# The high halves of 38 probability tiles, from VectorE to ScalarE, in a sparse-attention layer

## The chip, the cores and the metric

The kernel runs on one core of a Trainium2 chip. A core has TensorE (matmuls, PE in the profile, its weight loads PEld), VectorE (DVE), ScalarE (ACT), GpSimd (POOL) and SyncE (SP, which issues most of the DMAs). The metric is the device time of one execution in microseconds; several runs are made and their median is taken.

## The reference

One inference step of a layer with two token mixers. What matters here is mixer A on the prompt (1024 tokens, 8 heads of 64 in 2 groups g of 4, which share keys and values):

```
s_s = einsum('bqgrd,bgqnld->bqgrnl', qg, k_sel) * scale     # selected blocks of 64 keys
p_s = softmax(where(m_s, s_s, NEG));  o_s = p_s @ v_sel
s_w = einsum('bqgrd,bkgd->bqgrk', qg, kw) * scale           # window of 512 keys
p_w = softmax(where(m_w, s_w, NEG));  o_w = p_w @ vw
o_a = gw[..., 0] * o_c + gw[..., 1] * o_s + gw[..., 2] * o_w
```

A third branch, o_c, works on compressed keys and gives the scores by which the blocks are selected. The mixer's output is gated (SiLU), projected, merged with mixer B through sigmoid gates (g_a, g_b), and projected once more (w_out). All of it is float32.

## The kernel before

To be as exact as float32 and as fast as the quicker format FR (float32r), the kernel splits an operand into a high half, rounded to FR, and a low half, the rest, and sums the products of the halves. A split is two instructions: a copy into FR (the high half) and a subtraction (the low half).

The attention goes over 16 tiles (g, i), i being a block of 128 queries. For each, `front` makes the queries' transposes (R, R2), finds the maxima of the scores (matmuls into PSUM banks of the tag mx, in which the masks of the edges are added by an FR matmul of an identity, `ident_r`, with a table, `edges`; VectorE reduces them to bm and wm) and selects the blocks (imp, BT). `scores` then goes through the spans (w, k) of the tile, first the window's (w = 1), then the selected blocks' (w = 0), 132 in all: two matmuls into a PSUM bank st (two banks), an exponential on ScalarE into pt (four buffers), and, where the span lies on an edge, a mask on GpSimd (40 of the 132). For each span `low` splits the probabilities into `p2[:, 0]` and `p2[:, 1]`, and `outputs` adds three matmuls with the values into a bank pv. `weigh` and `close` scale and sum the branches (sr, u, f). `n` is the span's number in its tile, and n % 3 says which engine makes the halves: the high half is made by VectorE where n % 3 = 2 (38 spans) and by ScalarE elsewhere (94); the low half by GpSimd where n % 3 = 1 (44) and by VectorE elsewhere (88).

The profile leaves out the numbers of buffers, so that p2 reads p, R2 reads R, L1 and L2 read L, and s4 and s8 read s. All instructions carry line 216, the proxy that records them, so they are told apart by their tiles.

The order of all instructions is set beforehand by a planner (`Plan`): every stream of work is a generator that yields what it waits for; the planner estimates each instruction's cost by engine and size, and takes next the stream whose data are ready first by its own account. Matmuls of the projections and gates (`ct_proj`, tiles mm<-hh,c0h and the like, 128x344, six at a time) are the filler: they are taken when the attention has nothing ready. When the last tile of g = 1 is closed, the merge is opened: `products` loads back what was spilled and splits it into xh and xl, and `merge_job` multiplies these with w_br_b and then w_br_a; the output projection follows. The engines run in order, each on its own list, and wait for each other by semaphores.

Of the kernel before, what the change touches and what calls it, by code (L numbers as in the profile page):

```python
# [13 lines left out]
AF = mybir.ActivationFunctionType  # L14
# [244 lines left out]
def nsa_gmlp_step(ctx: ExitStack, tc: tile.TileContext, a: dict):  # L259
    nc = tc.nc  # L260
    plan = Plan()
    dve, act, pool, pe, sp = (plan.engine(e, n) for e, n in (
        (nc.vector, "dve"), (nc.scalar, "act"), (nc.gpsimd, "pool"), (nc.tensor, "pe"), (nc.sync, "sp")))
# [1446 lines left out]
    def scores():  # L1710

        for g, i in TILES:
            yield lambda: (g, i) in got and "blocks" in built
            R, R2, pgT = got.pop((g, i))
            pgTs[g, i] = pgT
            Rf, R2f = R.rearrange("p r q -> p (r q)"), R2.rearrange("p r q -> p (r q)")
            for n, (w, k) in enumerate(spans(i)):
                yield lambda: waiting[0] < PT_BUFS
                yield bank_free("st")
                waiting[0] += 1  # L1720
                s = bank("st")
                sl = slice(k * 128, k * 128 + 128)
                pe.matmul(s, lhsT=L1[g, w][:, sl], rhs=Rf, start=True, stop=False)
                pe.matmul(s, lhsT=L2[g, w][:, sl], rhs=R2f, start=False, stop=True)
                pt = areg.tile([128, 512], F32, name="pt", bufs=PT_BUFS)
                act.activation(pt, s, AF.Exp, scale=0.125)
                if k == i or w and k == i - 4:
                    sign = 1 if k == i else -1
                    pool.affine_select(out=pt, in_=pt, pattern=[[0, 4], [sign, 128]], compare_op=OP.is_ge, fill=0.0,
                                       base=min(sign, 0), channel_multiplier=-sign)  # L1730
                plan.add(low(g, i, n, pt), 0)
            scored[0] += 1

    def low(g, i, n, pt):

        yield pt
        yield lambda: flying[0] < P_BUFS
        flying[0] += 1
        p2 = areg.tile([128, 2, 512], FR, name="p2", bufs=P_BUFS)
        if n % 3 in HI_DVE:  # L1740
            dve.tensor_copy(p2[:, 0], pt)
        else:
            act.activation(p2[:, 0], pt, AF.Copy)
        yield p2[:, 0]
        (pool if n % 3 in ON_POOL else dve).tensor_tensor(p2[:, 1], pt, p2[:, 0].bitcast(F32), op=OP.subtract)
        waiting[0] -= 1
        cut[g, i, n] = p2
# [24 lines left out]
            plan.add(close(g, i, pgTs.pop((g, i)), o), 0)  # L1772

    ON_POOL = (1,)
    HI_DVE = (2,)
    pgTs, cut = {}, {}
    waiting, flying, scored, open_ = [0], [0], [0], [0]

# [250 lines left out]
```

## Time and profile before

| | before |
|---|---|
| median of 3 runs (lowest to highest) | 1042.48 us (1041.79 to 1043.07) |
| profiled execution: time, span | 1042.65 us, 1041.0 us |
| PE busy | 1017.1 us, 98% |
| PEld busy | 887.8 us, 85% |
| DVE busy | 653.5 us, 63% |
| ACT busy | 468.6 us, 45% |
| POOL busy | 306.7 us, 29% |
| granted TensorE clock, mean | 0.998 |

The profile is one execution. Busy times are unions over an engine's instructions; a matmul's record runs from its start to its modelled end and overlaps the next, so a full PE row tells that work was always under way, not that none of it stood. The rows of waits are what tells that. An engine's idle time before an instruction is put down to the instruction that released it.

### The profile page before, as it was taken

The numbers are of one execution on the slowest core, as the hardware profiler recorded it, in microseconds if no ns is written. First come the engines' busy times: TensorE is split into PE (matmuls) and PEld (weight loads), VectorE is DVE, ScalarE is ACT, GpSimd is POOL, SyncE is SP. The second block draws the span as 40 slices with busy tenths as digits, with TensorE's granted clock in tenths as the row PEclk, the third lists the DMA queues.
The fourth block names the chain that finished last, engine by engine and source line by source line (L and its number), as shares of the span: only waits on it lengthen the run. The fifth ranks groups of instructions, "written<-read, shape, count | busy, mean of one in ns | idle before, by whom it ended". The sixth has DMA issues, their size and how long they took to land. (4 is left out here: it accounts for less than half of the span.)

```text
span 1041.0 us, 16320 instructions
## 1 busy us (share of the span) xinstructions
PE 1017.1 (98%) x5711; PEld 887.8 (85%) x5711; DVE 653.5 (63%) x1371; ACT 468.6 (45%) x984; POOL 306.7 (29%) x332
## 2 busy tenths in 40 slices
PE   7999999999999999999999999999999999999998
PEld 2589977879999999987888888878789999998776
DVE  4676786454668757477788568896843345575322
ACT  5774232001322245777766676667675331232000
POOL 0443574555231110013334332433343000251000
PEclk9999999999999999999999999999999999999999
DMA  9735451203874745421311121211123586554321
GB/s 320 249 115 175 135 183 43 71 21 113 285 216 143 261 147 195 132 67 55 92 56 46 57 72 48 63 29 51 30 68 89 184 246 202 173 159 143 123 90 63
DMA packets 106311, 130.33 MB, mean 125 GB/s; under 512 B 27299, under 2 KB 71525, under 8 KB 106230
## 3 DMA queue, kind: packets, MB, share of 16 engines
q1 hardware_dynamic: 101622, 112.52, 34.4%
q0 software_dynamic: 4608, 16.78, 5.3%
q8 instruction: 45, 0.74, 0.3%
q14 instruction: 36, 0.29, 0.1%
HBM read 98.95 MB, written 30.23 MB: 124 GB/s over the span
## 5 line engine op out<-in xcount | busy, mean ns | idle before, releaser
L216 PE MATMUL pv<-p,vv 128*128 128x512 f32 (+1 forms) x396 | 112.0, 398 | 0.1
L216 PE MATMUL mm<-hh,c0h 128*128 128x344 f32 x320 | 104.8, 327 | 0.0
L216 PE MATMUL mm<-hl,c0h 128*128 128x344 f32 x320 | 102.3, 320 | 0.0
L216 PE MATMUL mm<-hh,c0l 128*128 128x344 f32 x320 | 102.1, 319 | 0.0
L216 ACT ACTIVATE pt<-st 128x512 f32<-128x512 f32 x132 | 78.7, 596 | 51.0 <-PE st L216 49.7
L216 PE MATMUL mm<-hh,c1h 128*128 128x344 f32 x304 | 99.3, 326 | 0.0
L216 PE MATMUL mm<-hh,c1l 128*128 128x344 f32 x304 | 97.1, 319 | 0.0
L216 PE MATMUL mm<-hl,c1h 128*128 128x344 f32 x304 | 97.0, 319 | 0.0
L216 PE MATMUL st<-R,L 128*128 128x512 f32 (+1 forms) x264 | 87.1, 411 | 0.0
L216 PEld LDWEIGHTS pv<-p,vv 128*128 128x128 f32 (+1 forms) x396 | 65.0, 171 | 22.1 <-DVE p L216 1.9
L216 DVE TENSOR_TENSOR p<-pt,p 128x512 fp32r<-128x512 f32 x88 | 66.7, 766 | 11.3 <-ACT p L216 10.9
L216 POOL TENSOR_TENSOR p<-pt,p 128x512 fp32r<-128x512 f32 x44 | 59.1, 1343 | 45.1 <-ACT p L216 40.9
L216 ACT ACTIVATE p<-pt 128x512 fp32r<-128x512 f32 x94 | 59.1, 629 | 15.5 <-POOL pt L216 11.5
L216 PEld LDWEIGHTS mm<-hh,c0h 128*128 128x128 f32 x320 | 60.3, 188 | 2.9 <-issue 0.2
L216 PEld LDWEIGHTS mm<-hh,c0l 128*128 128x128 f32 x320 | 60.3, 188 | 2.3
L216 PEld LDWEIGHTS mm<-hl,c0h 128*128 128x128 f32 x320 | 60.1, 188 | 0.0
L216 PEld LDWEIGHTS mm<-hh,c1h 128*128 128x128 f32 x304 | 57.2, 188 | 2.8 <-issue 0.2
L216 PEld LDWEIGHTS mm<-hh,c1l 128*128 128x128 f32 x304 | 57.2, 188 | 2.2
L216 PE MATMUL mx<-L,R 128*128 128x512 f32 (+3 forms) x204 | 55.8, 340 | 2.8 <-DVE bm L216 2.1
L216 POOL TENSOR_SCALAR_AFFINE_SELECT pt<-pt 128x512 f32<-128x512 f32 x40 | 27.4, 684 | 105.6 <-ACT pt L216 102.7
L216 PEld LDWEIGHTS mm<-hl,c1h 128*128 128x128 f32 x304 | 57.1, 188 | 0.0
L216 POOL TENSOR_TENSOR m<-m,th 128x344 f32<-128x344 f32 x24 | 25.0, 1062 | 108.4 <-DVE th L216 108.4
(501 smaller groups left out, 2701.7 us busy)
## 6 DMA issues: line engine op xcount, KB each, us to landing
t_db<-th SPq DMA_DIRECT2D x24, 172.0 KB
t_da<-th SPq DMA_DIRECT2D x24, 172.0 KB
th<-t_db SPq DMA_DIRECT2D x24, 172.0 KB
th<-t_da SPq DMA_DIRECT2D x24, 172.0 KB
graw<-in_w_ada_dram SPq DMA_DIRECT2D x16, 256.0 KB
araw<-in_w_ada_dram SPq DMA_DIRECT2D x16, 256.0 KB
xt<-in_x_dram SPq DMA_DIRECT2D x8, 512.0 KB
eraw<-in_w_ada_dram SPq DMA_DIRECT2D x16, 256.0 KB
```

Source lines behind the costliest of these rows:

```text
L216: r = getattr(real, name)(*args, **kw)
```

## The change

The choice by n % 3 falls away for the high half: ScalarE makes all 132 of them, with the same activation (a copy) as the 94 before. Who makes the low half stays as it was (GpSimd for n % 3 = 1, VectorE for the others), and so do all buffers.

```
@@ -1737,10 +1737,7 @@
         yield lambda: flying[0] < P_BUFS
         flying[0] += 1
         p2 = areg.tile([128, 2, 512], FR, name="p2", bufs=P_BUFS)
-        if n % 3 in HI_DVE:
-            dve.tensor_copy(p2[:, 0], pt)
-        else:
-            act.activation(p2[:, 0], pt, AF.Copy)
+        act.activation(p2[:, 0], pt, AF.Copy)
         yield p2[:, 0]
         (pool if n % 3 in ON_POOL else dve).tensor_tensor(p2[:, 1], pt, p2[:, 0].bitcast(F32), op=OP.subtract)
         waiting[0] -= 1
@@ -1772,7 +1769,6 @@
     ON_POOL = (1,)
-    HI_DVE = (2,)
     pgTs, cut = {}, {}
```

Since the planner counts the copies, it also sorts the rest of the attention anew. The list of VectorE, before, in the second tile (p_5367 is the p2 of a span with n % 3 = 2; c1l is the low half of a filler's weights; wm and bm are the maxima):

```order
L216 TENSOR_TENSOR p_5294<-pt,p_5294 128x512
L216 TENSOR_REDUCE wm<-mx 128x4 x2
L216 TENSOR_TENSOR c1l<-cr,c1h 128x512 x2
L216 CAST p_5367<-pt 128x512
L216 TENSOR_REDUCE wm<-mx 128x4
L216 TENSOR_REDUCE bm<-mx 128x8
L216 TENSOR_TENSOR p_5367<-pt,p_5367 128x512
L216 TENSOR_TENSOR p_5391<-pt,p_5391 128x512
L216 TENSOR_TENSOR u<-mx,u 128x256
```

The same place on VectorE after the change, where the span has become p_5345:

```order
L216 TENSOR_REDUCE wm<-mx 128x4 x2
L216 TENSOR_TENSOR p_5293<-pt,p_5293 128x512
L216 TENSOR_REDUCE wm<-mx 128x4
L216 TENSOR_REDUCE bm<-mx 128x8
L216 TENSOR_TENSOR p_5345<-pt,p_5345 128x512
L216 TENSOR_REDUCE bm<-mx 128x8 x2
L216 TENSOR_TENSOR u<-mx,u 128x256
L216 TENSOR_TENSOR p_5383<-pt,p_5383 128x512
```

The cast is gone, and the split of the filler's weights (c1l, twice) has moved to another place. On ScalarE the same place before, from the exponentials (pt<-st) and copies of this tile:

```order
L216 ACTIVATE p_5294<-pt 128x512
L216 ACTIVATE pt<-st 128x512
L216 ACTIVATE th<-mm 128x344
L216 ACTIVATE p_5326<-pt 128x512
L216 ACTIVATE pt<-st 128x512
L216 ACTIVATE sr<-pv 1x512
L216 ACTIVATE u<-pv 64x256 x2
L216 ACTIVATE pgT<-mx 128x128
L216 ACTIVATE c1h<-cr 128x512 x2
L216 ACTIVATE pt<-st 128x512
```

and after:

```order
L216 ACTIVATE p_5293<-pt 128x512
L216 ACTIVATE pt<-st 128x512
L216 ACTIVATE p_5315<-pt 128x512
L216 ACTIVATE pt<-st 128x512
L216 ACTIVATE th<-mm 128x344
L216 ACTIVATE pgT<-mx 128x128
L216 ACTIVATE p_5345<-pt 128x512
L216 ACTIVATE sr<-pv 1x512
L216 ACTIVATE u<-pv 64x256 x2
L216 ACTIVATE pt<-st 128x512
```

Between the exponential and the next one stands now the copy p_5345, with th and pgT ahead of it and sr and u behind it; c1h has moved away with c1l. On TensorE, at the end of the attention, the last three matmuls with the values before (mm are the filler's):

```order
L216 MATMUL mm<-hl,c1h 128x344
L216 MATMUL pv<-p_9196,vv_4490 128x512
L216 MATMUL pv<-p_9196,vv_4490 64x512
L216 MATMUL pv<-p_9196,vv_4490 128x512
L216 MATMUL mm<-hh,c1h 128x344
```

and after:

```order
L216 MATMUL mm<-hl,c0h 128x344
L216 MATMUL pv<-p_9262,vv_4490 128x512
L216 MATMUL pv<-p_9262,vv_4490 64x512
L216 MATMUL pv<-p_9262,vv_4490 128x512
L216 MATMUL mm<-hh,c0h 128x344
```

They stood at the rows 3896 to 3898 of TensorE's list and stand at 3942 to 3944; 720 of the filler's matmuls stood between the first scores and the last pv, and now 768, while the first matmul of the merge (st<-xh) stood at row 4219 and stands at 4217.

## Rows read from the trace of the kernel before

**Rows 1.** The page: its first line, and TensorE's share of the span.
```profile
span 1041.0 us, 16320 instructions
...
PE 1017.1 (98%) x5711; PEld 887.8 (85%) x5711; DVE 653.5 (63%) x1371; ACT 468.6 (45%) x984; POOL 306.7 (29%) x332
```

**Rows 2.** Busy time by window: length, PE, PEld, DVE, ACT, POOL, clock, DMA.
```profile
450.00:800.00 350.00, 343.85 (x1914) 295.10 (x1913) 253.78 (x570) 247.04 (x522) 127.83 (x140) 1.00 0.19 54
800.00:875.00 75.00, 75.00 (x481) 75.00 (x481) 32.72 (x67) 23.57 (x49) 4.34 (x6) 1.00 0.70 216
```

**Rows 3.** Waits of the weight loads, 450 to 800 us: total, times, longest.
```profile
PEld mx L216 <- DVE bm L216: 5.4, 10, 1.4
PEld mx L216 <- DVE wm L216: 2.8, 4, 1.4
...
PEld pv L216 <- DVE p L216: 1.9, 5, 0.5
PEld mx L216 <- ACT s L216: 1.7, 1, 1.7
PEld mx L216 <- DVE u L216: 0.9, 2, 0.8
...
PEld mx L216 <- ACT p L216: 0.4, 1, 0.4
PEld mx L216 <- ACT R L216: 0.2, 1, 0.2
```

**Rows 4.** Waits of the matmuls themselves, 450 to 800 us.
```profile
PE mx L216 <- DVE BT L216: 1.3, 1, 1.3
```

**Rows 5.** Waits of ScalarE, 450 to 800 us.
```profile
ACT pt L216 <- PE st L216: 49.7, 68, 3.1
...
ACT p L216 <- POOL pt L216: 11.5, 17, 1.3
```

**Rows 6.** Groups by form, 450 to 800 us: count, busy us, mean ns, idle before.
```profile
L216 ACT ACTIVATE pt<-st 128x512 f32<-128x512 f32 x132 | 78.7, 596 | 51.0 <-PE st L216 49.7
L216 DVE TENSOR_TENSOR p<-pt,p 128x512 fp32r<-128x512 f32 x88 | 66.7, 766 | 11.3 <-ACT p L216 10.9
L216 ACT ACTIVATE p<-pt 128x512 fp32r<-128x512 f32 x94 | 59.1, 629 | 15.5 <-POOL pt L216 11.5 <-PE pv L216 2.7
...
L216 DVE CAST p<-pt 128x512 fp32r<-128x512 f32 x38 | 21.3, 561 | 13.0 <-ACT pt L216 12.0 <-PE pv L216 1.0
```

**Rows 7.** Tile p: shortest, median, longest ns; first and last start.
```profile
L216 PE MATMUL pv<-p,vv x396: 387/393/502, 454.3 to 796.9; 128*128 128x512 f32 x132, 128*64 128x512 f32 x66
...
L216 DVE TENSOR_TENSOR p<-pt,p x88: 676/684/1727, 453.2 to 791.1; 128x512 fp32r<-128x512 f32 x88
...
L216 DVE CAST p<-pt x38: 410/420/1554, 459.4 to 785.5; 128x512 fp32r<-128x512 f32 x38
```

**Rows 8.** In order of time, 478 to 484 us: start, duration, instruction [idle before].
```profile
478.80 2.10 DVE L216 TENSOR_TENSOR c1l<-cr,c1h 128x512 fp32r<-128x512 f32 x2 [1.95 <-ACT c1h L216]
...
480.43 1.06 POOL L216 TENSOR_TENSOR u<-u 128x256 f32<-128x256 f32 x1
...
480.82 0.96 DVE L216 CAST p<-pt 128x512 fp32r<-128x512 f32 x1
...
481.70 0.68 DVE L216 TENSOR_REDUCE wm<-mx 128x4 f32<-128x512 f32 x1
...
482.44 0.71 PE L216 MATMUL mx<-pgT,vc 128*128 128x128 f32 x4 [1.00 <-DVE wm L216]
...
482.81 1.27 POOL L216 TENSOR_TENSOR p<-pt,p 128x512 fp32r<-128x512 f32 x1 [1.31 <-ACT p L216]
482.90 1.73 DVE L216 TENSOR_TENSOR p<-pt,p 128x512 fp32r<-128x512 f32 x1
```

**Rows 9.** In order of time, VectorE: the last xl of branch b.
```profile
834.42 0.52 DVE L216 SCALAR_TENSOR_TENSOR xl<-zt,xh 128x344 fp32r<-128x344 f32 x1 [0.61 <-ACT xh L216]
```

**Rows 10.** Tile xh: the matmuls that read it first.
```profile
L216 PE MATMUL st<-xh,c0h x32: 316/319/323, 848.0 to 925.5; 128*128 128x344 f32 x32
```

More of the change, by code (lines that the diff above doesn't have):

```diff
@@ L1739, in low @@
         p2 = areg.tile([128, 2, 512], FR, name="p2", bufs=P_BUFS)
[L1740 to L1743, printed above, removed]
+        act.activation(p2[:, 0], pt, AF.Copy)
         yield p2[:, 0]
@@ L1774, in nsa_gmlp_step @@
     ON_POOL = (1,)
-    HI_DVE = (2,)
     pgTs, cut = {}, {}
```

## The prediction

> **What bounds the kernel now.** I read the page first for the engines' shares, then one window over the attention stage, then the waits of TensorE in that window, then the rows of the work that moves, and last one of the waits in order of time.
>
> TensorE is busy 1017.1 us of a span of 1041.0 us [rows 1]. The profiled execution took 1042.65 us, 1.65 us more than its span; it stands 0.17 us over the median of 1042.48 us, so a sum made against it holds for the median too. The moved copies lie between 459 and 786 us and the matmuls of the values (pv) between 454 and 797 us [rows 7], so I take 450 to 800 us as the attention stage [rows 2]. There TensorE is busy 343.85 of 350.00 us, VectorE 253.78, ScalarE 247.04 and GpSimd 127.83. Behind it, from 800 to 875 us, TensorE is busy 75.00 of 75.00 us with 481 matmuls: it has work without a gap. In the stage too there is always other work to give it: the projection matmuls (mm), which the planner strews between the attention's own.
>
> So nothing but TensorE's own rows can fill the stage, and the change touches none of them. What it can alter is how long TensorE stands still. The waits of its weight loads show where [rows 3]: 5.4 us and 2.8 us for VectorE's maxima (bm, wm, which free a PSUM bank of the tag mx), 1.9 us for the low halves (p), 0.9 us for u; with 1.3 us for BT in the matmuls' own rows [rows 4] that is 12.3 us for VectorE. For ScalarE they are 1.7, 0.4 and 0.2 us, together 2.3 us. None is for an exponential: on the contrary ScalarE waits 49.7 us in 68 places for the scores (st) [rows 5]. ScalarE is thus mostly ahead of TensorE, VectorE now and then behind it.
>
> **The change part by part.** *Removed:* 38 copies on VectorE (n % 3 = 2 among the 132 probability tiles; the row is CAST p<-pt x38), busy 21.3 us, mean 561 ns [rows 6]. The median of one is 420 ns and the longest 1554 ns [rows 7]: 38 times 141 ns, 5.4 us of the 21.3, is waiting inside the instruction. The low halves on VectorE show the same: median 684, mean 766, longest 1727 ns. The rows in order of time show at what [rows 8]: the copy that began at 480.82 us took 0.96 us while GpSimd's u<-u ran from 480.43 to 481.49, and the low half at 482.90 took 1.73 us over GpSimd's own low half, 482.81 to 484.08. The Trainium skill, page "SBUF — State Buffer", section "Who interferes with whom", names it: a VectorE copy of this kind, and a tensor_tensor with both inputs in SBUF, can be shut out by a GpSimd instruction for its whole length, and shut it out in turn. The trace agrees by the lengths just given. By this rule the 88 low halves that stay on VectorE go on colliding, 88 times 82 ns or 7.2 us, so only the copies' 5.4 us go; the sum below has no other number in it.
>
> *Added:* 38 copies on ScalarE, of a kind that is there already 94 times with a mean of 629 ns [rows 6]: 23.9 us more, 247.04 to 270.9 us of 350, or 77%. In the shown order the copy stands behind its exponential with two other instructions between them, and the exponentials queued behind it wait for it, and TensorE for them if both banks of st are full. Six of the 38 tiles are masked ones (i = 2 twice, i = 6 once, for both g), where ScalarE must stand until GpSimd's mask is done. The 34 masked copies that ScalarE has now stand 11.5 us in 17 waits [rows 5], 0.34 us each, so the six add 2.0 us.
>
> *Sum.* How often a queue is late grows, as an estimate, with its busy share over its idle share. For VectorE that is 253.78 / 96.22 = 2.64 before and, 21.3 us less, 232.5 / 117.5 = 1.98 after: a quarter less, so of the 12.3 us about 3.1 us go. The bounds are nothing (the copies stand where TensorE doesn't wait) and all 12.3 us. I take the quarter, because one of the waits bears it out: at 482.44 us TensorE had stood 1.00 us for wm, which VectorE began at 481.70 only after the 0.96 us copy [rows 8]; but in other waits no copy stands in the row. For ScalarE the shares are 247.04 / 102.96 = 2.40 and, with 23.9 and 2.0 us more, 272.9 / 77.1 = 3.54, so its 2.3 us become 3.4 us: 1.1 us lost. The bounds are nothing and 23.9 us, every moved copy delaying TensorE by its full length; I stay near the lower, as the nearest rows show no wait of TensorE for pt at all. Net: 3.1 less 1.1, **2.0 us less**, 1042.48 to about 1040.5 us.
>
> *The order.* The planner counts the copies too, so it re-sorts TensorE's rows: the last pv stands 48 mm matmuls later. This by itself costs nothing: 481 matmuls in 75.00 us [rows 2] are 156 ns each, so 48 are 7.5 us of filling that is done earlier and missing later. Later there is cover: the last pv starts at 796.9 us, the twelve halves xh, xl of branch b are done by 834.42 + 0.52 us, and the first matmul that reads them starts at 848.0 [rows 7, 9, 10]. The 13.1 us between shrink to 5.6. If that cover were gone, each missing microsecond would be one of TensorE's.
>
> **The rivals.**
> *Waits only change places (no gain).* The largest waits hang on collisions of low halves and of the projection's splits with GpSimd, which stay; a new order makes others of them. For it: the first matmuls behind the copy at 480.82 waited for maxima that were also behind a 2.10 us pair of c1l [rows 8]. Against it: VectorE has 21.3 us less to do for the same waits. Time: 1042.5 us, give or take 1.5.
>
> *ScalarE becomes late (slower).* In-order, an exponential stands behind a moved copy, and st's two banks are both waiting to be read. Of 132 exponentials [rows 6] 68 began by waiting for TensorE [rows 5] and can take a delay; 64 did not. If the 38 copies are spread evenly, 38 x 64 / 132 = 18.4 stand before those 64; at 629 ns that is 11.6 us of delay, and if TensorE feels half, 5.8 us, less the 3.1 us on VectorE: 1045.2 us. It decides from the point at which TensorE's waits for pt and p of ScalarE pass 3.1 us. Against it: no such wait for pt now.
>
> *Each copy is simply slower (slower).* ScalarE's mean of 629 ns stands against VectorE's median of 420 ns, what a copy takes when nothing shuts it out [rows 6, 7]. If each of the 38 chains from exponential to pv were on TensorE's path, 38 times 209 ns is 7.9 us: 1050.4 us. Against it: TensorE waited for p only 1.9 us in five places [rows 3]. The Trainium skill, page "ScalarE: Activation LUTs", section "Rules for kernel authors", would have it so: plain elementwise work belongs on VectorE, not on ScalarE. The two durations agree with it for one instruction; whether it is so for the kernel hangs on the row of five places.
>
> *All waits on VectorE go (much faster).* 12.3 less 1.1 is 11.2 us: 1031.3 us. Against it: the collisions that stay.
>
> **How the numbers follow.** Chances: a part of VectorE's waits goes, 0.48 (1038.5 to 1042.0); waits only change places, 0.24 (1041.0 to 1044.0, a little over at both ends); ScalarE late, 0.18 (1044 to 1047); each copy slower, 0.04; most of VectorE's waits go, 0.06 (1031 to 1038). 0.2% is 2.1 us, about what a measurement of this kernel can tell from no change. Of the first case a little over half lies below 1040.4 (0.26) and the rest within; of the second 0.06 below, 0.13 within, 0.05 above; of the third 0.16 above and 0.02 within. That makes faster 0.38, within 0.2% 0.37, slower 0.25. The forecast is that of the first case, 1040.5 us, at the edge of what can be told. The range for 8 in 10 leaves out most of the two small cases at the ends and a tail on each side: 1037.0 to 1046.0.
>
> **What would show it.** VectorE's busy time in the stage down by some 21 us, ScalarE's up by some 24; no CAST p<-pt; the weight loads' waits for bm, wm, p and u under 11.0 us, those for ScalarE a little over 2.3; the last pv later than 796.9 us by about 5; the stage from there to the merge without a gap. The prediction is wrong if TensorE's rows show waits for pt (ScalarE late), or waits for bm and wm of the old size behind other instructions (only places changed), or a wait for xl at the first merge matmul (cover gone).

## The result and the profile after

The changed kernel takes 1035.66 us (median of 4 runs, 1034.82 to 1036.76), the kernel before beside it 1042.61 us: a ratio of 0.9938, 95% interval 0.9926 to 0.995. That is 6.5 us less (5.2 to 7.7), where 2.0 were forecast and the range ended at 1037.0. The profiled execution took 1035.44 us.

The page of the changed kernel and its busy times by window (columns as in [rows 2]):

```profile
span 1033.7 us, 16312 instructions
...
PE 1014.0 (98%) x5711; PEld 888.8 (86%) x5711; DVE 634.3 (61%) x1333; ACT 488.9 (47%) x1022; POOL 304.1 (29%) x332
```

```profile
450.00:800.00 350.00, 346.99 (x1947) 301.35 (x1946) 233.18 (x529) 268.14 (x562) 125.29 (x140) 1.00 0.19 56
800.00:875.00 75.00, 75.00 (x482) 75.00 (x481) 35.01 (x72) 22.98 (x49) 4.32 (x6) 1.00 0.71 218
```

The work moved as said: in the stage VectorE has 20.6 us less, ScalarE 21.1 us more. TensorE got through 33 more matmuls in the same 350 us (1947 against 1914).

Waits of the weight loads, of the matmuls and of ScalarE in 450 to 800 us (total, times, longest), to be laid beside [rows 3 to 5]:

```profile
PEld mx L216 <- PE pv L216: 2.6, 3, 1.0
PEld mx L216 <- issue: 1.8, 5, 0.5
PEld pv L216 <- DVE p L216: 1.4, 3, 0.8
PEld mx L216 <- DVE bm L216: 1.0, 4, 0.4
PEld mx L216 <- DVE wm L216: 1.0, 3, 0.5
PEld mx L216 <- ACT s L216: 0.8, 1, 0.8
PEld mx L216 <- ACT th L216: 0.6, 1, 0.6
PEld mx L216 <- DVE u L216: 0.5, 2, 0.3
PEld mx L216 <- ACT L L216: 0.2, 1, 0.2
```

```profile
PE mx L216 <- DVE BT L216: 1.6, 3, 0.6
```

```profile
ACT pt L216 <- PE st L216: 29.6, 47, 1.6
...
ACT p L216 <- POOL pt L216: 11.0, 19, 1.3
```

The weight loads wait 3.9 us for VectorE's bm, wm, p and u, where they waited 11.0: not a quarter less but two thirds. For ScalarE they wait 1.6 us, less than the 2.3 before, and never for pt. The exponentials stand less for TensorE's scores (29.6 us against 49.7): ScalarE's slack paid for the copies.

Groups by form in the stage, after (count, busy us, mean ns, idle before), beside [rows 6], and then the two groups of the filler's low halves before:

```profile
L216 ACT ACTIVATE p<-pt 128x512 fp32r<-128x512 f32 x132 | 83.0, 629 | 13.9 <-POOL pt L216 11.0 <-PE pv L216 1.0
...
L216 DVE TENSOR_TENSOR p<-pt,p 128x512 fp32r<-128x512 f32 x88 | 66.9, 765 | 25.8 <-ACT p L216 25.6
...
L216 DVE TENSOR_TENSOR c0l<-cr,c0h 128x512 fp32r<-128x512 f32 x10 | 6.7, 711 | 5.3 <-ACT c0h L216 5.2
L216 DVE TENSOR_TENSOR c1l<-cr,c1h 128x512 fp32r<-128x512 f32 x10 | 6.4, 683 | 5.9 <-ACT c1h L216 5.9
```

```profile
L216 DVE TENSOR_TENSOR c1l<-cr,c1h 128x512 fp32r<-128x512 f32 x10 | 9.1, 949 | 8.3 <-ACT c1h L216 8.3
...
L216 DVE TENSOR_TENSOR c0l<-cr,c0h 128x512 fp32r<-128x512 f32 x10 | 8.6, 897 | 6.5 <-ACT c0h L216 6.4
```

The 88 low halves of the probabilities are as long as they were (765 ns against 766): their collisions with GpSimd stayed. The filler's splits are not: 20 instructions that took 17.7 us take 13.1, though the change does not touch them.

Where the time went is read from the first score matmul and the first matmul of the merge. Tiles R and xh, first before ([rows 10] has its xh, 848.0), then after, with first and last start at the end:

```profile
L216 PE MATMUL st<-R,L x264: 388/396/483, 450.1 to 791.7; 128*128 128x512 f32 x132
```

```profile
L216 PE MATMUL st<-R,L x264: 388/397/484, 448.3 to 792.2; 128*128 128x512 f32 x132
...
L216 PE MATMUL st<-xh,c0h x32: 316/320/323, 841.0 to 918.4; 128*128 128x344 f32 x32
```

From the one to the other it took 848.0 - 450.1 = 397.9 us before and 841.0 - 448.3 = 392.7 after, 5.2 less; I call this the attention's stretch. The spans differ by 7.3 us; 1.8 of it lie ahead of the stretch, where the instructions are the same in both (the lists differ first behind the first score, TensorE's some sixty matmuls behind it). A difference of that size there tells nothing: in eleven profiles with this same beginning, taken on several chips, the first score came between 446.5 and 450.1 us.

The last matmuls with the values, after:

```profile
L216 PE MATMUL pv<-p,vv x396: 386/394/500, 452.5 to 797.4; 128*128 128x512 f32 x132, 128*64 128x512 f32 x66
```

The last of them starts 349.1 us behind the first score, where it was 346.8 before ([rows 7]). It comes 2.3 us later, although 48 more of the filler's matmuls stand ahead of it, by the forecast's estimate 7.5 us of work.

### The profile page after: what moved, and what is told of

Read it like the earlier page. It is cut to its first block, busy times and chain, and to the rows that moved or that the text cites. A ratio compares the mean times of both kernels' runs of the same rounds, so it can differ in the third digit from the quotient of the medians.

```text
span 1033.7 us, 16312 instructions
## 1 busy us (share of the span) xinstructions
PE 1014.0 (98%) x5711; PEld 888.8 (86%) x5711; DVE 634.3 (61%) x1333; ACT 488.9 (47%) x1022; POOL 304.1 (29%) x332
## 5 line engine op out<-in xcount | busy, mean ns | idle before, releaser
L216 ACT ACTIVATE p<-pt 128x512 fp32r<-128x512 f32 x132 | 83.0, 629 | 13.9 <-POOL pt L216 11.0
```

The source lines that it names most:

```text
L216: r = getattr(real, name)(*args, **kw)
```

## The experiments

Eighteen runs were made, e1 to e18. Ratios are to the kernel before on the same chip, with 95% intervals in brackets.

### Engine and order apart

The planner books an instruction on an engine and so sets the order. In e1 the 38 copies run on ScalarE but are booked on VectorE, which leaves every list but the copies' as before; in e2 it is the other way round, the changed kernel's order with the copies on VectorE. e5 is the changed kernel again.

```
e1:  nc.scalar.activation(p2[:, 0], pt, AF.Copy)
     plan.op("dve", "tensor_copy", [p2[:, 0]], [pt])
e2:  nc.vector.tensor_copy(p2[:, 0], pt)
     plan.op("act", "activation", [p2[:, 0]], [pt])
```

> The 38 copies run on ScalarE, but the planner still books them on VectorE at VectorE's cost, so every other instruction stands where it stood before the change. Theory (VectorE has less to do, so its maxima come sooner): most of the 7.0 us gain, 1035.5 to 1038 us, and waits of the weight loads for VectorE at 4 to 6 us, as against 11.0 before and 3.9 after. Rival (the new order of TensorE's rows made the gain): 1041 to 1044 us, waits for VectorE still 9 us or more. If each gives about half: 1038 to 1040 us.

> The reverse: the order of the changed kernel, planned as if the 38 copies ran on ScalarE, but they run on VectorE. Theory (work on VectorE): 1041 to 1044 us, waits for VectorE about 10 us. Rival (order): 1035 to 1037.5 us, waits for VectorE 4 to 5 us.

> The changed kernel unaltered, beside the kernel before on the same chip as the runs of this call. If the first comparison holds: 0.9938 of before, within 0.0015. If its size was a chance of the chip or of the runs: 0.996 to 0.998, near what the engine alone (0.9989) and the order alone (0.9982) gave together, 0.997.

e1: 0.9989 (0.998 to 0.9998). e2: 0.9982 (0.9973 to 0.9991). e5: 0.9942 (0.9926 to 0.9959). So the engine alone is worth 1.1 us, the order alone 1.9, both together over 6: more than the two added up. The stage's window in e1 and its largest waits of the weight loads for VectorE and ScalarE, with the one of the matmuls for BT, tell why so little came of the engine:

```profile
450.00:800.00 350.00, 344.05 (x1918) 296.15 (x1917) 236.65 (x531) 267.84 (x560) 126.33 (x140) 1.00 0.18 55
```

```profile
PEld mx L216 <- DVE bm L216: 4.5, 8, 1.2
...
PEld pv L216 <- DVE p L216: 1.6, 4, 0.6
PEld mx L216 <- ACT pt L216: 1.3, 1, 1.3
PEld mx L216 <- ACT R L216: 1.3, 3, 0.6
PEld mx L216 <- DVE wm L216: 1.1, 2, 0.6
...
PE mx L216 <- DVE BT L216: 1.6, 3, 0.9
```

VectorE has 17 us less to do than before, and bm still holds TensorE up for 4.5 us; VectorE's waits as the prediction adds them up (bm, wm, p, u and BT) come to 8.8 us, against 12.3 before. ScalarE's come to 2.6 us, for pt and R, where they were 2.3 for s, p and R. The splits still collide (c0l 8.3 us, c1l 8.0).

### The same pair in other orders

One number of the planner, `LATE["dve"]` (127 ns), is set to 147 or 107. That re-sorts the whole program from its early stages on, not the attention alone. e3 and e4 are the kernel before and the changed one with 147, e11 and e10 with 107. e7 is e4's order with the copies on VectorE, e8 is e3's with the copies on ScalarE, made as e2 and e1 were.

```
-    LATE = {"pe": 196.0, "dve": 127.0, "act": 170.0, "pool": 100.0}
+    LATE = {"pe": 196.0, "dve": 147.0, "act": 170.0, "pool": 100.0}
```

> The kernel before with one number of the planner altered, VectorE's results 147 instead of 127 ns late: same engines for all work, another order. It tells what an order alone is worth. Theory (work on VectorE): within 2 us of 1042.6. Rival (the order decides): it may lie anywhere in 1036 to 1046 us.

> The changed kernel with the same number altered, 147 instead of 127 ns. Theory (work on VectorE): within 2 us of 1035.7. Rival (the changed kernel's order was a lucky one): 1038 to 1043 us.

> The order of the jittered changed kernel (planned for ScalarE, 147 ns), with the 38 copies run on VectorE. With ScalarE it had 1.0019 of before. Theory (in a given order the copies on ScalarE are worth 1 to 3 us): 1.003 to 1.005. Rival (they are worth nothing, only orders differ): 1.001 to 1.0025; if they cost: under 1.001.

> The order of the jittered kernel before (planned for VectorE, 147 ns), with the 38 copies run on ScalarE. With VectorE it had 1.0005 of before. Theory (worth 1 to 3 us in a given order): 0.9975 to 0.9995. Rival (worth nothing): 1.0 to 1.0015.

> The changed kernel with the planner's due time for VectorE set to 107 ns instead of 127: a third order planned for the copies on ScalarE. Theory (the change is worth 1 to 5 us on average and an order plus or minus 4 us): 0.994 to 1.002, below the kernel before with the same 107 in the next run by 1 to 6 us. Rival (the change is worth its 6.5 us in any order): 6 to 7 us below the next run.

> The kernel before with the planner's due time for VectorE set to 107 ns instead of 127: the partner of the run with the changed kernel at 107. Theory (orders differ by some us whatever the engine): 0.997 to 1.003 of before. Rival (the order of before is a good or a bad one by nature): within 0.1% of before, as at 147.

| planner's number | copies by n % 3 (as before) | all on ScalarE (as after) | difference |
|---|---|---|---|
| 127 | 1 | 0.9938 (0.9926 to 0.995) | -6.5 us |
| 147 | e3: 1.0005 (0.9996 to 1.0014) | e4: 1.0019 (1.0009 to 1.0028) | +1.5 us |
| 107 | e11: 1.0068 (1.005 to 1.0086) | e10: 1.0048 (1.003 to 1.0066) | -2.1 us |

The same edit gains 6.5, loses 1.5 or gains 2.1 us, on average 2.4 us of gain; at 107 the two intervals overlap, so that the 2.1 is hardly told from nothing. With the order held still the engine's part is steadier: in orders planned for the old engines ScalarE gains 1.1 us (e1) and 0.9 (e8, 0.9996, 0.9987 to 1.0006, against e3); in orders planned for ScalarE it gains 4.6 (after against e2) and 5.3 (e4 against e7, 1.007, 1.0053 to 1.0087). The 0.9 of e8 can't be told from nothing.

### The filler's splits

Four of the larger waits of TensorE in the kernel before stand behind a split of the filler's weights. One was in [rows 8] (c1l, 2.10 us, TensorE's wait 1.00). GpSimd's part there, and then the other three, in order of time, in the kernel before, with what GpSimd did meanwhile:

```profile
478.46 1.89 POOL L216 TENSOR_TENSOR u<-u,f 128x256 f32<-128x256 f32 x2
...
522.18 1.19 POOL L216 TENSOR_TENSOR u<-u,f 128x256 f32<-128x256 f32 x1
522.86 2.21 DVE L216 TENSOR_TENSOR c0l<-cr,c0h 128x512 fp32r<-128x512 f32 x2
523.45 1.07 POOL L216 TENSOR_TENSOR u<-u 128x256 f32<-128x256 f32 x1
525.72 0.71 PE L216 MATMUL mx<-pgT,vc 128*128 128x128 f32 x4 [0.54 <-DVE bm L216]
...
689.57 1.48 POOL L216 TENSOR_TENSOR p<-pt,p 128x512 fp32r<-128x512 f32 x1 [0.21 <-ACT p L216]
689.83 1.77 DVE L216 TENSOR_TENSOR c1l<-cr,c1h 128x512 fp32r<-128x512 f32 x1
692.86 0.55 PE L216 MATMUL mx<-L,R 128*128 128x128 f32 x2 [0.97 <-DVE bm L216]
...
733.39 1.30 POOL L216 TENSOR_TENSOR p<-pt,p 128x512 fp32r<-128x512 f32 x1 [0.75 <-PE mx L216]
733.78 2.05 DVE L216 TENSOR_TENSOR c0l<-cr,c0h 128x512 fp32r<-128x512 f32 x2
736.49 0.50 PE L216 MATMUL mx<-L,R 128*128 128x512 f32 x1 [0.56 <-DVE bm L216]
```

After the change a pair stands where GpSimd has nothing to do, and takes 1.29 us:

```profile
486.39 1.29 DVE L216 TENSOR_TENSOR c1l<-cr,c1h 128x512 fp32r<-128x512 f32 x2 [3.25 <-ACT c1h L216]
```

Against 1.29 us for a pair and 0.68 for one, the three are 0.92, 1.09 and 0.76 us too long, and TensorE then waited 0.54, 0.97 and 0.56 us: each wait is smaller than what the collision ahead of it added. The next kernels, in the order of before, are meant to take this collision away. e6 gives the low halves c0l and c1l to GpSimd itself, e9 to ScalarE, e16 leaves them on VectorE in a form with one input. In e9 and e16 (and in e13 to e15 below) the low half becomes a rounded copy of the raw weight, so the computation of the filler's low halves is left out; in e9 and e16 these are 22 instructions in all.

```
-                split(h, l, r)
+                act.activation(h, r, AF.Copy)
+    e6:         nc.gpsimd.tensor_tensor(l, r, h.bitcast(F32), op=OP.subtract)
+    e9:         nc.scalar.activation(l, r, AF.Copy)
+    e16:        nc.vector.tensor_reduce(l, r[:, :, :, None], op=OP.max, axis=AX.X)
+                plan.op("dve", "tensor_tensor", [l], [r, h])
```

> The kernel before, with the low halves of the filler's weights (c0l, c1l; 20 in the attention stage) made by GpSimd, while the planner books them on VectorE as before, so that no other instruction moves; the 38 copies stay on VectorE. In the trace of before four of the five largest waits of TensorE in the stage stand behind a c0l or c1l that took 1.06 to 1.77 us beside a GpSimd instruction; in the new order these 20 take 13.1 us instead of 17.7. Theory (the new order gains because these splits no longer collide): 2.5 to 4 us faster than before, ratio 0.996 to 0.9975. Rival (they merely stood near the waits): 0.999 to 1.002.

> The kernel before in its own order; of the filler's weights, the low halves c0l and c1l of the attention stage (20 instructions) are made by ScalarE as a copy of the raw weights instead of by VectorE as a subtraction, so these low halves are not computed; VectorE then has no long split to collide with GpSimd. Theory (the largest of TensorE's waits for bm and wm stand behind a collided split, so a good part of the gain of the change is that the new order keeps the splits away from GpSimd): bm and wm waits of the weight loads fall from 8.2 us to under 5, time 0.996 to 0.9975 of before. Rival (the splits are bystanders; the order helps through where the chains stand): waits of the same size behind other instructions, 0.999 to 1.002.

> The kernel before in its own order; the low halves c0l and c1l of the attention stage are made on VectorE by a maximum over an axis of one element of the raw weights (so these low halves are not computed): one input only, about as long as an undisturbed split (the maxima of 128x512 have a mean of 682 ns against the splits' median of 694 and 789). Theory A (a split costs by its collisions with GpSimd): 0.994 to 0.997, near e9. Theory B (a split costs by standing in VectorE's list, two of 0.7 us in a row ahead of a maximum): 0.998 to 1.001.

e6: 1.0106 (1.0089 to 1.0123). It missed its aim: a split takes GpSimd 1431 to 1488 ns, and the low halves queued behind it came late (weight loads wait 6.0 us for GpSimd's p). e9: 0.9943 (0.9925 to 0.9961). e16: 0.9939 (0.9921 to 0.9957). Both reach the time of the changed kernel with the copies left where they were, and e9 gains more than its theory gave. In e16 the place of [rows 8] in order of time, VectorE, GpSimd and TensorE, then the window and the weight loads' waits:

```profile
475.10 1.27 DVE L869 TENSOR_REDUCE c1l<-cr 128x512 fp32r<-128x512 f32 x2
476.29 0.84 DVE L216 CAST p<-pt 128x512 fp32r<-128x512 f32 x1
477.05 0.68 DVE L216 TENSOR_REDUCE wm<-mx 128x4 f32<-128x512 f32 x1
...
476.81 1.61 POOL L216 TENSOR_TENSOR u<-u,f 128x256 f32<-128x256 f32 x2
...
479.61 0.61 PE L216 MATMUL mx<-pgT,vc 128*128 128x128 f32 x4
```

```profile
450.00:800.00 350.00, 347.79 (x1949) 300.57 (x1949) 250.74 (x571) 247.79 (x525) 128.41 (x143) 1.00 0.20 58
```

```profile
PEld mx L216 <- DVE bm L216: 3.0, 9, 0.6
...
PEld mx L216 <- DVE wm L216: 1.0, 2, 0.6
```

The pair takes 1.27 us instead of 2.10, and the matmul that had waited 1.00 us for wm does not wait. The other three splits in e16, and the one of the three matmuls behind them that still waits for bm:

```profile
518.29 1.27 DVE L869 TENSOR_REDUCE c0l<-cr 128x512 fp32r<-128x512 f32 x2
683.35 1.27 DVE L869 TENSOR_REDUCE c1l<-cr 128x512 fp32r<-128x512 f32 x2
686.73 0.55 PE L216 MATMUL mx<-L,R 128*128 128x128 f32 x2 [0.19 <-DVE bm L216]
727.33 1.26 DVE L869 TENSOR_REDUCE c0l<-cr 128x512 fp32r<-128x512 f32 x2
```

The matmuls' waits there were 0.54, 0.97 and 0.56 us and are nothing, 0.19 and nothing. VectorE's busy time fell by 3.0 us only, and the kernel by 6.3 us; in e1 it fell by 17.1 us and the kernel by 1.1. It is not how much VectorE has to do that counted here but which of its instructions are late. One reservation: a low half that is a copy does not need the high half either, so e9 and e16 also take away VectorE's waits for ScalarE's c0h and c1h (14.7 us in six places before, of which 1.95 at [rows 8]). In the other three places above no such wait stands ahead of the split, so there the collision is at fault; for the whole sum of some 6 us the two were not told apart. The changed kernel kept most of these waits of VectorE (5.2 and 5.9 us in the groups above) and gained all the same.

### Is it one gain or two, and the copies in the new order

e13 is the changed kernel with e9's edit, e14 is e2 with it, e15 is e11 with it. e17 is e2 with the copies as a maximum over one element: the same values, one input, longer. e12 is the changed kernel with the planner told that a 512 wide subtraction on VectorE takes 82 ns more; e18 the changed kernel with the filler's split planned in two steps with six matmuls between them.

```
e17: nc.vector.tensor_reduce(p2[:, 0], pt[:, :, None], op=OP.max, axis=AX.X)
     plan.op("act", "activation", [p2[:, 0]], [pt])
e12: return 67 + (0.52 if plain else 1.042) * size + (82 if name == "tensor_tensor" and size >= 512 else 0)
e18: if cut and nxt:
         nxt.split(1)
     yield t
```

> The changed kernel in its own order, and of the filler's weights the low halves c0l and c1l of the attention stage made by ScalarE as a copy of the raw weights (so these low halves are not computed), as in e9. Theory (the change gained by keeping the splits out of the way of bm and wm; with the splits gone nothing of it is left to gain twice): 0.992 to 0.996 of before, within 1.5 us of the changed kernel. Rival (two gains that add up): 0.987 to 0.990, about 6 us below the changed kernel.

> The order of the changed kernel with the copies left on VectorE (as e2), and the splits of the attention stage on ScalarE as in e9 (low halves not computed). Theory (what a copy on VectorE costs in this order it costs by delaying other instructions, splits among them, so without the splits most of e2's distance to the changed kernel goes): 0.993 to 0.996. Rival (the copies themselves are late for TensorE in this order): stays at e2's 0.998, at least over 0.997.

> The kernel of e11 (before with 107 ns, 1.0068) in its own order, with the splits of the attention stage on ScalarE (low halves not computed). Theory (orders differ by where they put the splits): most of e11's loss goes, 0.995 to 1.000. Rival (orders differ by something else, such as where the attention's own chain is cut): 1.003 to 1.007.

> The order of the changed kernel with the copies on VectorE as in e2, but made by a maximum over an axis of one element (the same values, one input; the maxima of 128x512 have a mean of 682 ns against the copies' 420 undisturbed and 461 on average in e2): no collision, but 38 times 221 ns, 8.4 us, longer on VectorE. Theory (in this order too it is the collisions that cost): 0.993 to 0.996. Rival (it is the copies' time in VectorE's list, or the wait for them): 0.998 or more, as e2 or slower.

> The changed kernel with the planner's cost of a 512 wide subtraction on VectorE raised by 82 ns, the mean length that collisions with GpSimd add (mean 766 less median 684). Theory (order matters, and a planner that is told the true length finds one at least as good): 0.990 to 0.996 of before. Rival (the order that the changed kernel got was a lucky draw among such orders): 0.996 to 1.002.

> The changed kernel with the filler's split of eight weight tiles planned in two steps of four, with six of the filler's matmuls planned between them, so that the planner can let maxima pass between the two low halves. A new order of everything, nothing left out. Theory (long pairs of splits ahead of bm and wm cost): 0.990 to 0.995 of before. Rival (any new order is a draw): 0.995 to 1.004.

e13: 0.9962 (0.9947 to 0.9976), two microseconds above the changed kernel, just outside the theory's range and far from the rival's. No second gain shows: the weight loads' waits for bm and wm are 1.5 us, where the changed kernel has 2.0. But the edit has a price of its own in this order, for ScalarE now makes the low halves too: the waits for ScalarE's pgT, L and s are 3.5 us against 1.6 for all of ScalarE's in the changed kernel, those for p 3.1 against 1.4. e16's form, which leaves ScalarE alone, was not run in the new order. e14: 0.9982 (0.9971 to 0.9993), as e2: as the rival had it, the gain that I expected if the copies cost by delaying splits did not come, though the price seen in e13 may hide a part of it. e15: 1.0087 (1.0068 to 1.0105), no better than e11: nothing here says that this order is bad by its splits, and the reason stays open. e17: 1.0004 (0.9995 to 1.0014): without collisions the copies cost more, not less, for they are longer. Its copies and its two largest waits for VectorE:

```profile
L1741 DVE TENSOR_REDUCE p<-pt x38: 669/677/689, 458.3 to 791.2; 128x512 fp32r<-128x512 f32 x38
```

```profile
PEld mx L216 <- DVE bm L216: 4.9, 11, 1.0
...
PEld mx L216 <- DVE wm L216: 3.2, 10, 0.7
```

In e2 these waits were 3.3 and 2.1 us with copies of 461 ns, in the changed kernel 1.0 and 1.0 with none. So in the new order it is the copies' time in VectorE's list that TensorE feels. e12: 0.9982 (0.9972 to 0.9992). e18: 1.0028 (1.0018 to 1.0038). Neither beats the changed kernel; both fit the rival that an order is a draw. Of the five orders planned with all copies on ScalarE (the changed kernel, e4, e10, e12, e18: 0.9938, 1.0019, 1.0048, 0.9982, 1.0028) the changed kernel's is the best by far, and three are slower than the kernel before. That the planner happened on this one is luck, which the size of the gain rests on.

The stretch from the first score to the first matmul of the merge, read as above from one profile each, goes with the ratios of all kernels that share the beginning to within 1.3 us, so that no larger part of a difference has to be sought outside it:

| kernel | order of | copies on | filler's low halves | stretch, us | ratio |
|---|---|---|---|---|---|
| before | before | VectorE | collide | 397.9 | 1 |
| e1 | before | ScalarE | collide | 397.3 | 0.9989 |
| e9 | before | VectorE | on ScalarE | 392.9 | 0.9943 |
| e16 | before | VectorE | one input | 392.4 | 0.9939 |
| e6 | before | VectorE | on GpSimd | 409.1 | 1.0106 |
| after, e5 | after | ScalarE | undisturbed | 392.7, 392.8 | 0.9938, 0.9942 |
| e2 | after | VectorE | undisturbed | 395.0 | 0.9982 |
| e17 | after | VectorE, longer | undisturbed | 397.8 | 1.0004 |
| e14 | after | VectorE | on ScalarE | 396.7 | 0.9982 |
| e13 | after | ScalarE | on ScalarE | 394.6 | 0.9962 |

## Why the prediction was wrong

The direction and the place were right, the size was not: 2.0 us forecast, 6.5 measured. Step by step:

*Removed, added.* Right. VectorE has 20.6 us less in the stage (some 21 forecast), ScalarE 21.1 more (some 24), a copy there takes 629 ns. The forecast that the 88 low halves would go on colliding held: 766 and 765 ns. It is what the Trainium skill, page "SBUF — State Buffer", section "Who interferes with whom", says of a subtraction with both inputs in SBUF. That a maximum with one input is left alone, which the same section says for trn2, agrees with e16 and e17: none of the 22 and 38 maxima took over 689 ns.

*The sum: "a quarter less, so of the 12.3 us about 3.1 us go".* For the change as a whole this term was too small: the waits for VectorE fell from 12.3 to 5.5 us, 6.8 less. For the engine's part alone it held: in e1, the order held still, they fell by 3.5 us to 8.8, and the time by 1.1 us (0.2 to 2.1), which the forecast's net 2.0 would have fitted. A share of busy over idle time treats all of VectorE's work alike, and every instruction as staying where it stood. What it left out is that in the old order some six microseconds hung on some twenty splits (e9, e16), and that the change would move them.

*The order: "this by itself costs nothing".* This is the step that failed: the new order stands in the sum with nothing. With the copies on ScalarE it is worth 5.3 us (0.9938 against e1's 0.9989), most of the 6.5. I looked at it for its price at the merge alone, and that part was right: the last xl ends at 836.8, the merge starts at 841.0, 4.2 us of cover are left (5.6 forecast) and no wait stands there. But I did not look for its gain. The rows on record before the result showed it: c1l, twice, had moved away from the place where [rows 8] had it collide. The rival "waits only change places" even named the splits' collisions as the cause of the largest waits, and then took it that they "stay". The splits' part of them went, by the order: e2 has the splits undisturbed as well (13.1 us). The low halves' part stayed.

*ScalarE's 1.1 us lost.* Wrong sign: the weight loads' waits for ScalarE are 1.6 us against 2.3, and the masked copies' wait for GpSimd stayed at 11.0 us (11.5) where 2.0 more were forecast. In e1, without the new order, ScalarE's waits were 2.6 us: 0.3 lost, not 1.1.

*The rivals.* ScalarE late: refuted here, no wait for pt; in the order of before (e1) there was one of 1.3 us. Each copy simply slower: refuted. The Trainium skill, page "ScalarE: Activation LUTs", section "Rules for kernel authors", prefers VectorE for relu, max, min, add and mul; that a plain copy goes with these is how the prediction took it. The instruction is slower on ScalarE, 629 ns against 420 undisturbed; with the order held still the kernel was faster with it in each pair but one (e8 against e3), where no difference could be measured. Waits only change places: false of this pair, true of the pair at 147 (VectorE's waits, added up the same way, 9.0 us in e3 and 9.7 in e4). All of VectorE's waits go: half true (6.8 of 12.3). None of the signs that were to show the prediction wrong came: it was wrong by a gain that it had not looked for.

*What is shown and what stays open.* Shown: the gain is in the attention's stretch, to about a microsecond; the engine alone gives 1.1 us of it and the rest needs the new order; the old order loses some 6 us to the filler's splits as they stand in it; the new order has them undisturbed; that order pays in full only with the copies on ScalarE. Shown at three places only: that it is the splits' collision and not their wait for the high half. Not shown: that the 6.5 us of the change are these 6 us of the splits. Undisturbed splits are not enough for a gain: with the copies on VectorE e2 has them and gains 1.9 us, and with the copies on ScalarE e4 has them nearly so (c0l 685 ns on average, c1l 730, where e3 has 905 and 706) and is slower than e3. Open: why one order bears the copies on VectorE (e9, e16) and the other does not (e2, e14), and what makes the orders at 147 and 107 slower.

## What to carry to other kernels

Where a planner or scheduler sorts by cost, an edit has two effects, its own and a new order's; hold the order still (book the instruction as before, run it elsewhere) before crediting the edit, and expect of a single re-sorting some microseconds of either sign: here the edit's own worth in the old order is 1.1 us, and the same edit in three planned orders gave -6.5, +1.5 and -2.1. Price an engine's waits from what stands ahead of each of the largest ones, not from its busy share: 3 us taken from the right instructions, with their waits for the high halves (e16), gained some six times what 17 us taken from others did (e1). And when the lists before and after are at hand, look up where those very instructions now stand.

## What the runs showed of the hardware

A subtraction that met a GpSimd instruction held up both: in [rows 8]'s place the pair of splits took 2.10 us and GpSimd's pair of u<-u,f beside it 1.89, and with a one-input form in its stead 1.27 and 1.61 (GpSimd's pair then ran beside a copy of 0.84 us). The time ahead of the attention, the same instructions each time, varied by 3.6 us between profiles (446.5 to 450.1 us), so that a difference of that size between the spans of two profiles said nothing here.
